# Row maxima of a 64 MB array: contiguous 2 MB loads in place of a 512 KB partition pitch, with the results turned by 32x32 block transposes before the store

## Chip, core and metric

The kernel runs on one core of one Trainium2 chip. The metric is the device time of one execution in microseconds (us). The span of a profile, which is also quoted, runs from the first to the last instruction of that core.

## The reference, cut to what matters

```python
def setup_inputs():
    batch, seq, dim = 32, 512, 1024
    return {"x": np.random.randn(batch, seq, dim).astype(np.float32)}

def reference(x):
    return np.max(x, axis=-1).astype(np.float32)
```

There are 16384 rows of 4 KB, 67.1 MB to read, and one float32 per row to write (64 KB).

## The kernel before

Partition p owns the 128 rows p*128 to p*128+127, which is 512 KB of x. A bulk tile takes four consecutive rows of every partition (16 KB each, 2 MB in all). The last 16 rows of every partition come in eight tiles of 1 MB. The results of a partition are consecutive in the output, so they can be stored as they are.

```python
    I = N // P                                        # 128 rows a partition
    xr = xf.rearrange("(p i) d -> p i d", p=P)        # partition pitch 512 KB
    out_r = bass.AP(tensor=of.tensor, offset=of.offset, ap=[[I, P], [1, I]])
    GB = 4; GT = 2; TAIL_ROWS = 16                    # NB = 28, NT = 8, SPLIT = 112
    # pools: bulk bufs=10, tailp bufs=5, res bufs=1
    # ... (cut)
    for c in range(NB):
        b = c * GB
        xc = bulk.tile([P, GB, D], mybir.dt.float32)
        nc.sync.dma_start(out=xc, in_=xr[:, b:b + GB, :])
        nc.vector.reduce_max(out=res[:, b:b + GB], in_=xc, axis=mybir.AxisListType.X)

    nc.scalar.dma_start(out=out_r[:, :SPLIT], in_=res[:, :SPLIT])       # 56 KB

    for t in range(NT):
        b = SPLIT + t * GT
        xt = tailp.tile([P, GT, D], mybir.dt.float32)
        nc.sync.dma_start(out=xt, in_=xr[:, b:b + GT, :])
        nc.vector.reduce_max(out=res[:, b:b + GT], in_=xt, axis=mybir.AxisListType.X)

    nc.scalar.dma_start(out=out_r[:, SPLIT:], in_=res[:, SPLIT:])       # 8 KB, 64 B runs
```

Of the kernel before, what the change touches and what calls it, by code (L numbers as in the profile page):

```python
# [1 line left out]

# [4 lines left out]


@with_exitstack  # L10
def kernel(
    ctx: ExitStack,
    tc: tile.TileContext,
    x: bass.AP,
    out: bass.AP,
):
    nc = tc.nc
    P = 128

    xf = x.flatten_outer_dims()  # L20
    N, D = xf.shape
    assert N % P == 0
    I = N // P

    xr = xf.rearrange("(p i) d -> p i d", p=P)

    of = out.flatten_outer_dims()
    out_r = bass.AP(tensor=of.tensor, offset=of.offset, ap=[[I, P], [1, I]])

    GB = 4  # L30
    GT = 2
    TAIL_ROWS = 16
    NB = (I - TAIL_ROWS) // GB
    NT = TAIL_ROWS // GT
    SPLIT = I - TAIL_ROWS

    bulk = ctx.enter_context(tc.tile_pool(name="bulk", bufs=10))
    tailp = ctx.enter_context(tc.tile_pool(name="tailp", bufs=5))
    respool = ctx.enter_context(tc.tile_pool(name="res", bufs=1))

    res = respool.tile([P, I], mybir.dt.float32)

    for c in range(NB):
        b = c * GB
        xc = bulk.tile([P, GB, D], mybir.dt.float32)
        nc.sync.dma_start(out=xc, in_=xr[:, b:b + GB, :])  # L46
        nc.vector.reduce_max(  # L47
            out=res[:, b:b + GB],
            in_=xc,
            axis=mybir.AxisListType.X,  # L50
        )

    nc.scalar.dma_start(out=out_r[:, :SPLIT], in_=res[:, :SPLIT])

    for t in range(NT):
        b = SPLIT + t * GT
        xt = tailp.tile([P, GT, D], mybir.dt.float32)
        nc.sync.dma_start(out=xt, in_=xr[:, b:b + GT, :])
        nc.vector.reduce_max(  # L59
            out=res[:, b:b + GT],  # L60
            in_=xt,
            axis=mybir.AxisListType.X,
        )

    nc.scalar.dma_start(out=out_r[:, SPLIT:], in_=res[:, SPLIT:])


# [1 line left out]
_INS = ['x']  # L69
_OUTS = [((32, 512), 'float32')]  # L70


# [23 lines left out]
```

## Time and profile before

| | before |
|---|---|
| time, median of the runs at hand before the change was run | 166.98 us (166.93 to 167.51) |
| span of the profiled execution | 166.5 us |
| read from memory | 67.11 MB, 403 GB/s over the span |
| VectorE (DVE) busy | 141.4 us |
| distance of two bulk reductions, undisturbed | 4.89 us (2.097 MB / 4.89 us = 429 GB/s) |
| one bulk reduction | 4.42 us |

The first lines are of the page of the kernel before: the span, the busy time, the DMA rows in 40 slices of the span (each digit is the busy share of a slice in tenths), and the chain of work that ended last, by engine. SPq, ACTq and DVEq are the instruction queues of SyncE, ScalarE and VectorE; the first two issue the DMAs here.

```profile
span 166.5 us, 142 instructions
DVE 141.4 (85%) x36; POOL 0.2 (0%) x4
...
DMA  5999999999999999999999999999999999999950
GB/s 189 429 441 429 429 394 425 433 437 429 433 421 354 425 433 429 429 429 429 433 421 429 429 429 437 417 429 433 429 433 421 425 433 411 425 417 423 421 222 2
...
DMA 89%; DVE 8%; SPq 1%; issue 0%
```

The DMA engines are busy from the second slice to the last but two, and the chain that ends last is made of loads. Two slices stand out, 394 and 354 GB/s. The timeline of VectorE (start, duration, instruction, and in brackets the idle time ahead of it and what ended it) shows what they are:

```profile
22.90 4.42 DVE L47 TENSOR_REDUCE res<-xc 128x4 f32<-128x4096 f32 x1 [0.47 <-DMA xc<-in_x_dram]
28.43 4.42 DVE L47 TENSOR_REDUCE res<-xc 128x4 f32<-128x4096 f32 x1 [1.11 <-DMA xc<-in_x_dram]
33.29 4.42 DVE L47 TENSOR_REDUCE res<-xc 128x4 f32<-128x4096 f32 x1 [0.44 <-DMA xc<-in_x_dram]
...
52.86 4.42 DVE L47 TENSOR_REDUCE res<-xc 128x4 f32<-128x4096 f32 x1 [0.46 <-DMA xc<-in_x_dram]
58.61 4.42 DVE L47 TENSOR_REDUCE res<-xc 128x4 f32<-128x4096 f32 x1 [1.33 <-DMA xc<-in_x_dram]
63.50 4.42 DVE L47 TENSOR_REDUCE res<-xc 128x4 f32<-128x4096 f32 x1 [0.47 <-DMA xc<-in_x_dram]
```

VectorE always waits for the load, normally 0.47 us. Ahead of two tiles it waits 0.64 and 0.86 us longer, and this is never made good: all later tiles keep the old distance. The end of the same timeline:

```profile
141.82 4.42 DVE L47 TENSOR_REDUCE res<-xc 128x4 f32<-128x4096 f32 x1 [0.48 <-DMA xc<-in_x_dram]
146.16 15.47 DVE L59 TENSOR_REDUCE res<-xt 128x2 f32<-128x2048 f32 x7
...
161.80 2.29 DVE L59 TENSOR_REDUCE res<-xt 128x2 f32<-128x2048 f32 x1 [0.17 <-DMA xt<-in_x_dram]
164.12 0.34 ACTq L65 DMA_DIRECT2D out_dram<-res  x1
```

The last 2 MB tile leaves VectorE with a backlog, so seven tail reductions run without a gap. The eighth waits 0.17 us for its load. One store follows, and the span ends at 166.48 us, 2.36 us after that store's issue began.

### The profile page before, as it was taken

What the parts mean: (1) busy time and instruction counts of PE and PEld (TensorE: products, weight loads), DVE (VectorE), ACT (ScalarE), POOL (GpSimd) and SP (SyncE); (2) the same over time, 40 slices, a digit from 0 to 9 for tenths busy, and PEclk for the clock granted to TensorE, in tenths of its full rate; (3) what the DMA queues carried; (4) which work ended last, traced back from release to release, by engine and by line L of the source; (5) the groups of instructions that cost most, each with busy time, mean ns of one, the idle gap of its engine ahead of it and who ended that gap; (6) DMA issues with size and microseconds to landing.
All of it is one profiled execution on the core that took longest, in us unless ns stands there. A gap on an engine that the chain in (4) does not pass through costs nothing.

```text
span 166.5 us, 142 instructions
## 1 busy us (share of the span) xinstructions
DVE 141.4 (85%) x36; POOL 0.2 (0%) x4
## 2 busy tenths in 40 slices
DVE  0098887898888798888898888899888889999994
POOL 0000000000000000000000000000000000000000
DMA  5999999999999999999999999999999999999950
GB/s 189 429 441 429 429 394 425 433 437 429 433 421 354 425 433 429 429 429 429 433 421 429 429 429 437 417 429 433 429 433 421 425 433 411 425 417 423 421 222 2
DMA packets 5472, 67.18 MB, mean 404 GB/s; under 512 B 864, under 2 KB 864, under 8 KB 864
## 3 DMA queue, kind: packets, MB, share of 16 engines
q1 hardware_dynamic: 5184, 67.11, 95.7%
q10 hardware_dynamic: 288, 0.07, 0.2%
HBM read 67.11 MB, written 0.07 MB: 403 GB/s over the span
## 4 chain that ended last, share of the span: by engine, by line
DMA 89%; DVE 8%; SPq 1%; issue 0%
DMA xc<-in_x_dram 84%; DMA xt<-in_x_dram 5%; DVE res L59 5%; DVE res L47 3%; SPq L46 1%
## 5 line engine op out<-in xcount | busy, mean ns | idle before, releaser
L47 DVE TENSOR_REDUCE res<-xc 128x4 f32<-128x4096 f32 x28 | 123.8, 4420 | 22.5 <-DMA xc<-in_x_dram 22.5
L59 DVE TENSOR_REDUCE res<-xt 128x2 f32<-128x2048 f32 x8 | 17.8, 2280 | 0.2 <-DMA xt<-in_x_dram 0.2
L80 POOL MEMSET const-bfloat16-1.0<- 128x1 bf16 x1 | 0.1, 103 | 0.0
L80 POOL MEMSET const-uint8-127<- 128x1 uint8 x1 | 0.1, 103 | 0.0
L80 POOL MEMSET const-float32-1.0<- 128x1 f32 x1 | 0.1, 100 | 0.0
L80 POOL MEMSET const-float32-0.0<- 128x1 f32 x1 | 0.1, 99 | 0.2 <-issue 0.2
## 6 DMA issues: line engine op xcount, KB each, us to landing
xc<-in_x_dram SPq DMA_DIRECT2D x28, 2048.0 KB, 39.1
xt<-in_x_dram SPq DMA_DIRECT2D x8, 1024.0 KB, 23.5
out_dram<-res ACTq DMA_DIRECT2D x1, 56.0 KB, 6.8
out_dram<-res ACTq DMA_DIRECT2D x1, 8.0 KB, 1.4
```

What stands on the lines that cost most here:

```text
L46: nc.sync.dma_start(out=xc, in_=xr[:, b:b + GB, :])
L47: nc.vector.reduce_max(out=res[:, b:b + GB], in_=xc, axis=mybir.AxisListType.X,)
L59: nc.vector.reduce_max(out=res[:, b:b + GT], in_=xt, axis=mybir.AxisListType.X,)
L80: nc = _bacc.Bacc("TRN2", target_bir_lowering=False, num_devices=1)
```

## The change

Its intent: every bulk load should read one contiguous stretch of 2 MB, and not 128 pieces of 16 KB which lie 512 KB apart (this distance is what I call the pitch). The eight tail loads still read 128 pieces, of 8 KB, now 16 KB apart. The rows of a tile are then spread over the partitions (row = t*512 + p*4 + g), so the four results of one partition and tile are only 16 B of the output. To store longer runs, the results are transposed in blocks of 32x32, after which a partition holds 128 consecutive outputs (512 B), and four stores of 16 KB write them.

```diff
-    xr = xf.rearrange("(p i) d -> p i d", p=P)
+    xr = xf.rearrange("(t p g) d -> t p g d", p=P, g=G)
... (cut)
-        nc.sync.dma_start(out=xc, in_=xr[:, b:b + GB, :])
-        nc.vector.reduce_max(out=res[:, b:b + GB], in_=xc, ...)
+            nc.sync.dma_start(out=xc, in_=xr[t])
+            nc.vector.reduce_max(out=res[:, :, t], in_=xc, axis=X)
+        else:                                # the last four t, in halves
+                nc.sync.dma_start(out=xt, in_=xr[t, :, h:h + 2, :])
+                nc.vector.reduce_max(out=res[:, h:h + 2, t], in_=xt, axis=X)
-    nc.scalar.dma_start(out=out_r[:, :SPLIT], in_=res[:, :SPLIT])
-    nc.scalar.dma_start(out=out_r[:, SPLIT:], in_=res[:, SPLIT:])
+    for g in range(G):
+        nc.vector.transpose(out=turned[:, :, g], in_=res[:, g, :])
+    for q in range(P // 32):
+        dst = bass.AP(tensor=of.tensor, offset=of.offset + q * 32 * G,
+                      ap=[[P * G, T], [1, 32 * G]])
+        eng = (nc.scalar, nc.sync)[q % 2]
+        eng.dma_start(out=dst, in_=turned[q * 32:(q + 1) * 32, :, :].rearrange("p a g -> p (a g)"))
```

Number and size of the loads, bulk before tail, and the number of buffers stay as they were.

More of the change, by code (lines that the diff above doesn't have):

```diff
@@ L7 @@
 from concourse._compat import with_exitstack
+F32 = mybir.dt.float32
+G = 4
 @with_exitstack
@@ L18 @@
     P = 128
+    X = mybir.AxisListType.X
     xf = x.flatten_outer_dims()
     N, D = xf.shape
-    assert N % P == 0
-    I = N // P
-    xr = xf.rearrange("(p i) d -> p i d", p=P)
+    T = N // (P * G)
+    xr = xf.rearrange("(t p g) d -> t p g d", p=P, g=G)
     of = out.flatten_outer_dims()
-    out_r = bass.AP(tensor=of.tensor, offset=of.offset, ap=[[I, P], [1, I]])
-    GB = 4
-    GT = 2
-    TAIL_ROWS = 16
-    NB = (I - TAIL_ROWS) // GB
-    NT = TAIL_ROWS // GT
-    SPLIT = I - TAIL_ROWS
@@ L37 @@
     bulk = ctx.enter_context(tc.tile_pool(name="bulk", bufs=10))
     tailp = ctx.enter_context(tc.tile_pool(name="tailp", bufs=5))
-    respool = ctx.enter_context(tc.tile_pool(name="res", bufs=1))
-    res = respool.tile([P, I], mybir.dt.float32)
-    for c in range(NB):
-        b = c * GB
-        xc = bulk.tile([P, GB, D], mybir.dt.float32)
-        nc.sync.dma_start(out=xc, in_=xr[:, b:b + GB, :])
-        nc.vector.reduce_max(
-            out=res[:, b:b + GB],
-            in_=xc,
-            axis=mybir.AxisListType.X,
-        )
@@ L53 @@
-    nc.scalar.dma_start(out=out_r[:, :SPLIT], in_=res[:, :SPLIT])
-    for t in range(NT):
-        b = SPLIT + t * GT
-        xt = tailp.tile([P, GT, D], mybir.dt.float32)
-        nc.sync.dma_start(out=xt, in_=xr[:, b:b + GT, :])
-        nc.vector.reduce_max(
-            out=res[:, b:b + GT],
-            in_=xt,
-            axis=mybir.AxisListType.X,
-        )
-    nc.scalar.dma_start(out=out_r[:, SPLIT:], in_=res[:, SPLIT:])
+    once = ctx.enter_context(tc.tile_pool(name="once", bufs=1))
@@ new lines @@
+    res = once.tile([P, G, T], F32)
+    turned = once.tile([P, 32, G], F32)
+    for t in range(T):
+        if t < T - 4:
+            xc = bulk.tile([P, G, D], F32)
+            nc.sync.dma_start(out=xc, in_=xr[t])
+            nc.vector.reduce_max(out=res[:, :, t], in_=xc, axis=X)
+        else:
+            for h in range(0, G, 2):
+                xt = tailp.tile([P, 2, D], F32)
+                nc.sync.dma_start(out=xt, in_=xr[t, :, h:h + 2, :])
+                nc.vector.reduce_max(out=res[:, h:h + 2, t], in_=xt, axis=X)
@@ L69 @@
+    for g in range(G):
+        nc.vector.transpose(out=turned[:, :, g], in_=res[:, g, :])
+    for q in range(P // 32):
+        dst = bass.AP(
+            tensor=of.tensor,
+            offset=of.offset + q * 32 * G,
+            ap=[[P * G, T], [1, 32 * G]],
+        )
+        eng = (nc.scalar, nc.sync)[q % 2]
+        eng.dma_start(out=dst, in_=turned[q * 32:(q + 1) * 32, :, :].rearrange("p a g -> p (a g)"))
 _INS = ['x']
```

## The prediction

> **What bounds the kernel now.** The load stream. The page gives 67.11 MB read in a span of 166.5 us; its DMA row is at 9 tenths almost throughout, mostly 421-433 GB/s. In the timeline a 2 MB tile starts its reduction every 4.89 us (428.7 GB/s), while the reduction takes 4.42 us: VectorE idles about 0.47 us before each, always for the load. The chain of waits is 89% DMA. Two tiles are late: the one at 28.43 us by 0.64 us, the one at 58.61 us by 0.86 us (slices of 394 and 354 GB/s), 1.5 us in all. At the end VectorE is almost level with DMA: seven of eight 1 MB tail reductions run back to back, the eighth waits 0.17 us for its load and ends at 164.09 us; then come the 8 KB store (0.34 us issue, 1.4 us to landing) and 2.4 us in all to the end.
>
> **What the change leaves.** Number, size and order of the loads (28 of 2 MB, 8 of 1 MB), bytes per partition and load, buffers, reductions. VectorE's 141.4 us stays within 0.1 us; its 4-result writes become strided, nothing beside 4096 reads.
>
> **What it moves.** The pitch between partitions in x. The Trainium skill, page "DMA: Bandwidth & Descriptors", section "Latency and other measured facts", tells of DRAM copies of 128 x 16 KiB tiles at power-of-two pitches: 207 GB/s at 512 KiB against 214 at full rate, 3%. This trace shows little of that: every undisturbed tile takes 4.89 us to within 0.02 us, which looks like a ceiling of the engines, not like collisions. So I expect 4.87-4.90 us per tile after. What the pitch could own are the two late tiles. I give that a third: gain 1.5 us if so, expected 0.5 us.
>
> **What it removes.** The 56 KB store in the middle of the tail. Both stores together took 0.2% of the 16 engines' time (0.3 us): about 0.2 us off.
>
> **What it adds, all on the critical path, after the last reduction.** Four transposes of 128x32. None is in the trace; estimate from the reductions: 4420 - 2278 = 2142 ns for 2048 elements, so 136 ns fixed and 33 ns for 32 elements, 0.17 us each alone, about 0.09 us overlapped as the tail reductions are: 0.35-0.7 us. Then four 16 KB stores in 512 B runs, two on each of two queues: the second on a queue starts one issue (0.33-0.38 us) later; landing near the 1.4 us of the 8 KB store. Together +0.7 to +1.1 us.
>
> **Sum.** 166.98 + 0.9 - 0.2 - 0.5 = about 167.2 us; range 165.6 to 168.6. Faster by over 2%: 0.03; within 2%: 0.93; slower: 0.04.
>
> **What would show each step.** Timeline: bulk reductions still 4.89 us apart, whether late tiles remain; VectorE's idle time for loads near 22 us (21 if they go). Last reduction ending at 162.5-164.2 us. Four transposes of at most 0.2 us, first store 0.4-0.8 us after the last reduction, second pair about 0.35 us later, end of span 2.6-3.0 us after the first store's issue begins. Chain of waits: DMA still 88-89%.
>
> **What would make it wrong.** If the tile interval itself falls (a collision the same for each tile), to 4.82 us say, the stream gains 2.2 us, with the late tiles gone 3.7 us, just over 2%. If contiguous tiles make the sixteen engines meet in one part of the memory, the interval grows above 4.95 us and the kernel is slower. If transposes or 512 B stores cost 1 us apiece, it is slower by 2-3 us.

## The result, and the profile after

| | before | after |
|---|---|---|
| time, median (lowest to highest), 4 runs each | 166.98 us (166.93 to 167.51) | 168.13 us (168.01 to 168.24) |
| span of the profiled execution | 166.5 us | 166.3 us |
| VectorE busy | 141.4 us | 142.0 us |
| first reduction starts | 8.24 us | 8.58 us |
| last bulk reduction starts | 141.82 us | 140.72 us |
| last reduction ends | 164.09 us | 163.00 us |
| first of the closing stores issued | 164.12 us | 163.39 us |
| from there to the end of the span | 2.36 us | 2.95 us |

The ratio is 1.0059 with a 95% interval of 1.0044 to 1.0074. Ratios in this document are the mean time of one kernel's fast runs over the mean of the other's fast runs of the same rounds, so they are not quite the ratios of the medians that are quoted. The kernel after is slower by about half a per cent, within 2%.

The page of the kernel after, the same lines:

```profile
span 166.3 us, 147 instructions
DVE 142.0 (85%) x40; POOL 0.2 (0%) x4
...
DMA  5999999999999999999999999999999999999930
GB/s 177 402 433 437 441 437 429 410 426 441 433 429 414 426 441 433 426 414 429 441 433 422 422 426 441 433 422 422 426 441 433 422 418 418 422 424 420 422 154 16
...
DMA 83%; DVE 14%; SPq 1%; issue 0%; DVEq 0%
```

The two holes of before are gone. The next lines are of its VectorE timeline, first the start and the stretch in which before had its first late tile, then the end of the timeline of all engines:

```profile
8.58 4.42 DVE L44 TENSOR_REDUCE res<-xc 128x4 f32<-128x4096 f32 x1 [8.58 <-DMA xc<-in_x_dram]
...
23.23 4.42 DVE L44 TENSOR_REDUCE res<-xc 128x4 f32<-128x4096 f32 x1 [0.47 <-DMA xc<-in_x_dram]
28.13 4.42 DVE L44 TENSOR_REDUCE res<-xc 128x4 f32<-128x4096 f32 x1 [0.48 <-DMA xc<-in_x_dram]
```

```profile
140.72 4.42 DVE L44 TENSOR_REDUCE res<-xc 128x4 f32<-128x4096 f32 x1 [0.49 <-DMA xc<-in_x_dram]
145.06 15.44 DVE L49 TENSOR_REDUCE res<-xt 128x2 f32<-128x2048 f32 x7
160.53 0.33 DVE L52 STREAM_TRANSPOSE turned<-res 128x32 f32<-128x32 f32 x2
160.75 2.25 DVE L49 TENSOR_REDUCE res<-xt 128x2 f32<-128x2048 f32 x1
163.03 0.33 DVE L52 STREAM_TRANSPOSE turned<-res 128x32 f32<-128x32 f32 x2
163.39 0.83 SPq L61 DMA_DIRECT2D out_dram<-turned  x2
163.40 0.87 ACTq L61 DMA_DIRECT2D out_dram<-turned  x2
```

Every bulk tile is on time. Two of the transposes were scheduled ahead of the last reduction, because the rows that they turn were complete by then; they fill the 0.17 us in which before waited for its last load, so the last reduction no longer waits for a load, and the chain that ended last runs through VectorE for all eight tail reductions (14% in place of 8%).

Here is the puzzle: **the span fell by 0.14 us, and the time rose by 1.15 us.** The difference can be taken apart by stage from the two traces: first tile 8.58 - 8.24 = +0.34; the 27 further bulk tiles 132.14 - 133.58 = -1.44, nearly all of it the two late tiles; last bulk reduction to the end of the last reduction 22.28 - 22.27 = +0.01; from there to the first store +0.36; from the store to the end +0.59. The sum is -0.14 us. The stages at both ends cost 1.3 us, and the -1.44 us that hides them must be missing from the timed runs.

### The profile page after: what moved, and what is told of

The parts are those of the page before. It is cut to its first block, busy times and chain, and to the rows that moved or that the text cites. A ratio compares the mean times of both kernels' runs of the same rounds, so it can differ in the third digit from the quotient of the medians.

```text
span 166.3 us, 147 instructions
## 1 busy us (share of the span) xinstructions
DVE 142.0 (85%) x40; POOL 0.2 (0%) x4
## 4 chain that ended last, share of the span: by engine, by line
DMA 83%; DVE 14%; SPq 1%; issue 0%; DVEq 0%
DMA xc<-in_x_dram 83%; DVE res L49 11%; DVE res L44 3%; SPq L43 1%; DVE turned L52 0%; DVEq L87 0%
## 5 line engine op out<-in xcount | busy, mean ns | idle before, releaser
L52 DVE STREAM_TRANSPOSE turned<-res 128x32 f32<-128x32 f32 x4 | 0.7, 213 | 0.1
```

The costliest lines, as they stand in the source:

```text
L52: nc.vector.transpose(out=turned[:, :, g], in_=res[:, g, :])
```

## The experiments

Twelve builds were run (before and after again, eight other kernels, two of them twice), each on one chip and with runs of before between them. I call the chips A, B and C. Some kernels are wrong, which their expectation says: loads and end are exchanged separately, so the results land in other places.

| chip | kernel | loads | end | time, median (lowest to highest), runs | ratio to before, 95% interval |
|---|---|---|---|---|---|
| A | before | 512 KB pitch | old | 168.08 (167.47 to 169.16), 11 | |
| A | before, again | 512 KB pitch | old | 167.86 (167.28 to 169.41), 6 | 0.9987, 0.9942 to 1.0031 |
| A | contiguous, old end | contiguous | old | 167.21 (167.13 to 167.37), 6 | 0.9935, 0.9905 to 0.9965 |
| A | old loads, new end | 512 KB pitch | new | 168.81 (168.46 to 169.76), 8 | 1.0029, 0.9995 to 1.0063 |
| A | after, stores on one queue | contiguous | new, ACT only | 168.83 (168.79 to 169.05), 6 | 1.0033, 1.0002 to 1.0063 |
| B | before | 512 KB pitch | old | 166.82 (166.74 to 166.96), 9 | |
| B | after without transposes | contiguous | four stores | 167.56 (167.53 to 167.65), 5 | 1.0044, 1.0031 to 1.0056 |
| B | bulk reversed | 512 KB pitch | old | 166.83 (166.71 to 166.90), 5 | 0.9998, 0.9986 to 1.0011 |
| B | 128 KB pitch | 128 KB pitch | old | 166.44 (166.38 to 166.63), 5 | 0.9978, 0.9966 to 0.9991 |
| B | contiguous, first tile old | mixed | old | 166.82 (166.77 to 167.38), 5 | 0.9997, 0.9984 to 1.0011 |
| C | before | 512 KB pitch | old | 167.27 (166.75 to 167.57), 11 | |
| C | after, again | contiguous | new | 168.06 (167.96 to 168.18), 6 | 1.0053, 1.0038 to 1.0068 |
| C | contiguous, old end, again | contiguous | old | 167.12 (166.98 to 167.29), 6 | 0.9996, 0.9980 to 1.0013 |
| C | old loads, new end, again | 512 KB pitch | new | 167.92 (167.65 to 168.44), 6 | 1.0051, 1.0031 to 1.0071 |
| C | 128 KB pitch, fine tail | 128 KB pitch | old | 165.96 (165.89 to 166.71), 6 | 0.9936, 0.9917 to 0.9955 |

### 1. The kernel before, again

No edit.

> The kernel before, unchanged, under another label, to get span and time of several runs side by side. Theory P (the two late tiles of before belong to the 512 KB pitch): each profile of it shows two tiles 0.5-0.9 us late and the last reduction ending near 164.1 us. Rival N (the late tiles are chance): a second profile shows other tiles late, or none, with the last reduction ending near 162.7 us. The difference of time and span: after has 1.8 us (168.14 against 166.3); if the difference is the same here, spans would be near 165.2 us; if spans are near 166.0-166.5 us, the kernel after has 0.8 us or more outside its span. Ratio 1.000 +-0.002.

Its six runs lie between 167.28 and 169.41 us, and the eleven of the shared kernel before between 167.47 and 169.16. Every one of these runs has a span that is 1.8 us below its time: in the 105 runs that show both, the difference is 1.75 to 1.85 us for every kernel, before and after alike, but for four runs of the last kernel (up to 2.01 us). So nothing of the change lies outside the span, and the rival that said so (L in the next expectation) falls. What was odd was the profile of before: a span of 166.5 us belongs to an execution of about 168.3 us, slower than all its timed runs that I had. The second profile shows two other tiles late, at 37.97 us (by 0.43 us) and at 48.02 us (by 0.26 us). Which tiles are late is chance, as rival N says, but it is not a small matter: on this chip before scatters by 2 us.

```profile
37.97 4.42 DVE L47 TENSOR_REDUCE res<-xc 128x4 f32<-128x4096 f32 x1 [0.90 <-DMA xc<-in_x_dram]
...
48.02 4.42 DVE L47 TENSOR_REDUCE res<-xc 128x4 f32<-128x4096 f32 x1 [0.73 <-DMA xc<-in_x_dram]
```

The DMA packets of the trace show what a late tile is. A 16 KB packet most often takes 0.611 us, and sixteen are in flight on average. These are all packets of at least 4 KB that took over 0.7 us and started later than 7 us after the span began:

```
trace                        number  where (us)           how long (us)
before                          17   19, 23, 51           0.72 to 2.43
before, again                   15   33, 42-44            0.78 to 1.46
old loads, new end              16   23-25, 40            0.72 to 1.91
old loads, new end, again        8   23                   1.16 to 1.76
bulk reversed (chip B)           0
seven with a contiguous bulk      0
128 KB pitch, two traces         0
```

About eight packets at a time are held up, half of those in flight. (Before 7 us every trace has long packets, 16 to 27 of them; the longest is 1.36 to 1.60 us at the two larger pitches and 1.67 to 2.06 us in the seven with a contiguous bulk.) Each load completes in sixteen parts, here called shares, with one event each in the trace, and the reduction waits for the last of them: in the late tile of before it came at 28.41 us, and the reduction began at 28.43 us. In the trace of before the distance between the first and the last share of a tile steps from 0.66 us to 1.29 us at the first event and to 1.74 us at the second, and then stays. In this trace the shares that fell behind do not catch up. This is why a hold-up of some packets once moves the whole rest of the stream.

### 2. Contiguous loads, the old end

```diff
-    xr = xf.rearrange("(p i) d -> p i d", p=P)
+    xr = xf.rearrange("(t p g) d -> t p g d", p=P, g=4)
-        in_=xr[:, b:b + GB, :]
+        in_=xr[c]
-        in_=xr[:, b:b + GT, :]
+        in_=xr[b // 4, :, b % 4:b % 4 + GT, :]
```

> Wrong result on purpose (rows in another order): contiguous 2 MB loads, results and the two stores as before, no transposes. Theory P with an expensive end: 165.5 us (1.5 us less than before, no late tiles, difference of time and span about 1.0 us). Rival N: 167.0 us, as before. Rival L (contiguous loads cost something outside the span): 167.5-168 us with a difference of time and span of 1.8 us.

> Contiguous loads, old end, wrong on purpose, as in the run of that name. If the cost of the new end adds to whatever the loads do: 0.92 us (+-0.1) below the kernel after of the same call. If the contiguous loads have a later first tile on every chip: 0.2-0.4 us above the fastest runs of before of the same call.

On chip A it took 167.21 us with a range of only 0.24 us, while before scattered over 1.7 us beside it. On chip C it took 167.12 us, within a range of 0.31 us, against 166.75 to 167.57 us for before. None of the three readings of the first expectation was right as it stood: the loads do gain, against a before that is held up (ratio 0.9935 on A); they gain nothing against one that is not much so (0.9996 on C); and they lose 0.23 us to before's fastest run on C. The trace on C shows that loss at the start:

```profile
8.55 4.42 DVE L47 TENSOR_REDUCE res<-xc 128x4 f32<-128x4096 f32 x1 [8.55 <-DMA xc<-in_x_dram]
...
160.75 2.29 DVE L59 TENSOR_REDUCE res<-xt 128x2 f32<-128x2048 f32 x1 [0.17 <-DMA xt<-in_x_dram]
163.07 0.34 ACTq L65 DMA_DIRECT2D out_dram<-res  x1
```

In the six traces with contiguous bulk loads throughout the first reduction starts at 8.50 to 8.74 us (the seventh, with another first tile, is experiment 9), in the five at 512 KB pitch at 8.20 to 8.28 us. The steady distance is 4.89 to 4.90 us for both. The 0.17 us wait ahead of the last reduction is back: it belongs to the old end, with its store of 56 KB in the middle of the tail. (The kernel of experiment 8 has a store of only 8 KB there, and its eight tail reductions run without a gap.)

### 3. Old loads, the new end

```diff
 # in the kernel after
-    xr = xf.rearrange("(t p g) d -> t p g d", p=P, g=G)
+    xr = xf.rearrange("(p i) d -> p i d", p=P)
-                in_=xr[t]
+                in_=xr[:, t * G:(t + 1) * G, :]
-                in_=xr[t, :, h:h + 2, :]
+                in_=xr[:, t * G + h:t * G + h + 2, :]
```

> Wrong result on purpose: 512 KB pitch as before, transposes and four stores as after. Theory P with an expensive end: two late tiles, 168.5-169.5 us, difference of time and span near 1.8 us. Rival N: 168.1 us, as after. Rival L: 167.3-168 us with a difference of time and span of 1.0 us.

> 512 KB pitch with transposes and four stores, wrong on purpose. If the two costs add: 0.9 us (+-0.1) above before of the same call on a chip without stalls, and 0.2-0.4 us below the kernel after. On a chip with stalls its runs scatter by 1 us or more as before's do, and the kernel after's do not.

On chip A it scatters from 168.46 to 169.76 us. Its VectorE timeline has the late tiles that the kernel after, with the same end, does not have:

```profile
22.88 4.42 DVE L44 TENSOR_REDUCE res<-xc 128x4 f32<-128x4096 f32 x1 [0.48 <-DMA xc<-in_x_dram]
28.86 4.42 DVE L44 TENSOR_REDUCE res<-xc 128x4 f32<-128x4096 f32 x1 [1.56 <-DMA xc<-in_x_dram]
...
44.48 4.42 DVE L44 TENSOR_REDUCE res<-xc 128x4 f32<-128x4096 f32 x1 [1.43 <-DMA xc<-in_x_dram]
```

So hold-ups follow the loads and not the end. The end's price can be read with the loads held fixed. From the start of the last bulk reduction to the end of the span both traces of this kernel take 25.61 and 25.62 us, the kernel after 25.62 and 25.61 us on its two traces, and the six traces with before's two stores 24.65 to 24.67 us. The new end costs 0.95 us, whatever the loads do. In times of chip C it is 168.06 - 167.12 = 0.94 us with contiguous loads and 167.92 - 167.27 = 0.65 us at the old pitch; the second is blurred by the scatter, and between the fastest runs of each it is 167.65 - 166.75 = 0.90 us.

### 4. After, once more on chip C

No edit.

> The kernel after, unchanged, under another label, to have all four combinations of loads and end on one chip. On a chip whose runs of before do not scatter (before near 166.8 us): 168.0-168.1 us, that is +0.9 us for the end and +0.3 us for the later first tile. On a chip whose runs of before scatter up to 169 us: still 168.0-168.2 us, so no slower than before.

168.06 us, within 0.22 us: as expected, and as in the first comparison. The four corners of the square (two loads, two ends) are now measured on one chip. By the lowest runs they are 166.75 (before), 166.98 (new loads), 167.65 (new end), 167.96 us (both): +0.23 or +0.31 us for the loads, +0.90 or +0.98 us for the end. They add.

### 5. After, with all stores on one queue

```diff
-        eng = (nc.scalar, nc.sync)[q % 2]
+        eng = nc.scalar
```

> The kernel after with all four stores on the ACT queue. If the extra time outside the span comes from storing on two queues, the difference of time and span falls from 1.8 us to about 1.0 us; the span grows by two more issues one after the other, 0.7-0.8 us, so that the time is about 168.0-168.2 us. If it does not come from the two queues, time 168.7-169.0 us.

168.83 us, as its second reading expected, on chip A, where the kernel after was not run; against its 168.13 and 168.06 us elsewhere it is 0.7 to 0.8 us slower, the size of two further issues. The end of its timeline:

```profile
162.97 0.33 DVE L52 STREAM_TRANSPOSE turned<-res 128x32 f32<-128x32 f32 x2
163.33 1.78 ACTq L61 DMA_DIRECT2D out_dram<-turned  x4
```

Four issues take 1.78 us one after the other, against 0.83 and 0.87 us side by side; from the first issue to the end of the span it is 3.66 us against 2.95 us. Two queues are the better way to send four stores, and the number of stores one after the other on a queue is part of the price. The Trainium skill says in "DMA: Bandwidth & Descriptors", section "Issuing engines are not separate DMA queues", that issuing from several engines saves only the sequencer's issue time, usually small beside the DMA itself. This trace agrees on what is saved (0.71 us of span), and at the very end of this kernel, behind the last data, even that counts.

### 6. After, without its transposes

```diff
-    for g in range(G):
-        nc.vector.transpose(out=turned[:, :, g], in_=res[:, g, :])
-        eng.dma_start(out=dst, in_=turned[q * 32:(q + 1) * 32, :, :].rearrange("p a g -> p (a g)"))
+        eng.dma_start(out=dst, in_=res[q * 32:(q + 1) * 32, :, :].rearrange("p g t -> p (g t)"))
```

> The kernel after, its four transposes left out, the four stores taken from the untransposed results: wrong on purpose. Theory E (the new end costs 0.36 us through the transposes that stand between the last reduction and the first store, and 0.5 us through the stores): 0.5-0.6 us below the kernel after (two of the transposes also stand ahead of the last reduction, 0.22 us), so about 167.5-167.6 us; last reduction to start of first store 0.03 us; from there to the end of the span still 2.9 us. Rival S (the stores are nearly all of it): less than 0.2 us below the kernel after, about 168.0 us.

167.56 us, 0.50 to 0.57 us below the kernel after (on other chips; both kernels repeat within 0.25 us). Theory E holds, rival S falls. The end:

```profile
158.14 4.68 DVE L48 TENSOR_REDUCE res<-xt 128x2 f32<-128x2048 f32 x2
162.85 0.82 SPq L57 DMA_DIRECT2D out_dram<-res  x2
162.85 0.86 ACTq L57 DMA_DIRECT2D out_dram<-res  x2
```

The stores start 0.03 us after the last reduction in place of 0.39 us, and from there to the end it is 2.94 us, unchanged from after and 0.58 us longer than with the single 8 KB store of before. From the last bulk reduction to the end of the span this kernel takes 25.14 us, 0.48 us less than after and 0.48 us more than before. So the 0.95 us of the new end is half transposes and half stores. (For the stores it is 0.58 us less 0.1 us: with the store in the middle of the tail gone, and no transposes, the last reduction ends 0.1 us sooner after the last bulk reduction began, 22.18 us in place of 22.28 us.)

### 7. The old loads with the bulk reversed

```diff
-    for c in range(NB):
+    for c in reversed(range(NB)):
```

> The kernel before with its 28 bulk tiles loaded in reverse order; the result is correct. In the traces at 512 KB pitch so far, eight engines at a time had packets of 0.75-2.4 us in place of 0.61 us, at 23 and 51 us, at 33 and 42-44 us, at 23 and 40 us, never after 52 us. Theory T (the stalls belong to the time since the start): long packets again between 20 and 55 us only. Rival A (they belong to addresses, the first rows of each 512 KB): long packets between 85 and 130 us. Both: spans scatter over 1.5 us or more, as before, median time 167.5-168.5 us.

This run tells nothing about its question. On chip B there is no sign of hold-ups: before took 166.74 to 166.96 us in nine runs, this kernel 166.71 to 166.90 us, and its trace has no long packet after 7 us. Whether hold-ups belong to the time since the start or to addresses stays open. The run is of use all the same: its trace is the one at 512 KB pitch without a late tile, with a span of 165.04 us. That execution took 166.85 us, and the undisturbed before of the same chip took 166.82 us.

### 8. A pitch of 128 KB, the old end

```diff
-    I = N // P
-    xr = xf.rearrange("(p i) d -> p i d", p=P)
+    U = 4
+    I = N // P // U
+    xr = xf.rearrange("(u p i) d -> u p i d", u=U, p=P)
 # loop over u around the loop over bulk tiles; one store of 128 B runs after each of
 # the first three u; the last u has two stores of 64 B runs, its last 16 rows as before
```

> A correct kernel between the two: x in four groups of 4096 rows, partition pitch 128 KB in each, so results go out in 64-128 B runs without transposes, the last store as before. If the stalls need the pitch of 512 KB (or its 64 MB spread): no long packets after the first 6 us, runs within 0.4 us of each other, 167.1-167.3 us as with contiguous loads and the old end. If a pitch of 128 KB is enough for stalls: runs scatter over 1 us or more, median 167.5-168.2 us.

This kernel is correct, has no transposes, and took 166.44 us, ratio 0.9978 with an interval below 1. That is below both ranges that I had expected, neither of which foresaw an earlier first tile and a shorter end. Two lines of its timeline:

```profile
8.11 4.42 DVE L48 TENSOR_REDUCE res<-xc 128x4 f32<-128x4096 f32 x1 [8.11 <-DMA xc<-in_x_dram]
...
162.55 0.34 ACTq L64 DMA_DIRECT2D out_dram<-res  x1
```

Its first tile is the earliest of this chip (8.11 us against 8.28 us of before's loads), the closing store comes at 162.55 us against 162.68 us, and from there to the end it takes 2.20 us against 2.36 us. The shares of its first tile land within 0.51 us, against 0.74 us for the old pitch on the same chip and 0.70 us for contiguous loads. Its steadiness proves nothing, since before was as steady on this chip.

### 9. Contiguous, with only the first tile at the old pitch

```diff
 # in the kernel of experiment 2
-        in_=xr[c]
+        in_=xr[c] if c else xold[:, 0:GB, :]      # xold: the 512 KB pitch
```

> Contiguous loads with the old end (167.21 us on the chip of its run), only the very first tile read at the 512 KB pitch; wrong on purpose. If the 0.3-0.5 us by which the first tile lands later in contiguous loading (8.5-8.7 us against 8.2 us) come from the first tile's own pitch: first reduction at 8.2 us and time 166.8-166.9 us, the lowest yet. If they come from the next tiles that are in flight at the same time: first reduction at 8.5 us or later and time 167.1-167.3 us.

Inconclusive. Four of five runs took 166.77 to 166.85 us, as the first reading says and as before did. But the fifth, 167.38 us, is the profiled one, and it has the latest first tile of all traces:

```profile
8.78 4.42 DVE L49 TENSOR_REDUCE res<-xc 128x4 f32<-128x4096 f32 x1 [8.78 <-DMA xc<-in_x_dram]
```

There were no late tiles after that one, so all of its 0.6 us come from the start. The four good runs have no trace. So the times of four runs speak for the first reading and the only trace speaks against it. Whether the pitch of the first tile sets the start is not shown.

### 10. 128 KB pitch and a finer tail

In all kernels so far at least one reduction of a 1 MB tile is left to do when the last load lands: in before it lands at 161.78 us and its reduction ends 2.31 us later. This one keeps the 128 KB pitch and takes the last 12 MB as eight loads of 1 MB and eight of 512 KB.

```diff
-    TAIL_ROWS = 16
+    TAIL_ROWS = 24
+    LAST_ROWS = 8
+        pieces = [(b, GT, tailp) for b in range(split, I - LAST_ROWS, GT)]
+        pieces += [(b, 1, lastp) for b in range(I - LAST_ROWS, I)]
 # pools: bulk bufs=9, tailp bufs=4, lastp bufs=6; the middle store after the first 16 rows
```

> Correct kernel: pitch of 128 KB with the old end (166.44 us, 0.998 of before), and the last 12 MB in eight loads of 1 MB and eight of 512 KB in place of eight of 1 MB. The tail reductions of all kernels run back to back and the last one ends 2.3 us after the last load; with smaller last tiles VectorE should end about 1.2-1.4 us after it. Packets of 8 KB took 0.309 us against 0.611 us for 16 KB (1% more per byte), 4 KB packets should cost a little more: 0.2-0.4 us for 12 MB. Expected 165.6-165.9 us, ratio 0.993-0.995. If VectorE does not catch up (its idle before the last tile stays 0), or the small packets cost over 1 us: 166.4 us or more.

It is correct and the fastest: 165.96 us, ratio 0.9936 on chip C, just outside the expected 165.6 to 165.9 us. Part of that ratio is before's own scatter there; between the fastest runs it is 166.75 - 165.89 = 0.86 us. One of its six runs was 166.71 us, and it has no trace, so a hold-up in that run is not ruled out.

```profile
158.15 3.59 DVE L65 TENSOR_REDUCE res<-xt 128x1 f32<-128x1024 f32 x3
161.77 0.34 ACTq L70 DMA_DIRECT2D out_dram<-res  x1
```

The last load lands at 160.50 us and VectorE is done at 161.74 us, 1.24 us later in place of 2.31 us. The small packets give part of it back: a 4 KB packet most often takes 0.159 us, where a quarter of 0.611 us would be 0.153 us, and the last load lands 0.29 us later than in experiment 8 although the first tile was 0.14 us earlier.

## Why the prediction was right, and where its terms were off

The time, 168.13 us, lies in the range of 165.6 to 168.6 us, and "within 2%" was right. Both leave much room: the range is 3 us wide, and 2% is 3.3 us. The point, 167.2 us, was 0.9 us too low, and the missed terms below all erred in the same direction, so the range held in spite of them. One of the signs asked for did not come: the chain of waits has DMA at 83%, not 88 to 89%. Term by term:

- **The tile interval** was predicted to stay at 4.87 to 4.90 us, and stayed: 4.89 to 4.90 us at a pitch of 512 KB, 128 KB and 16 KB. A 16 KB packet took 0.611 us most often in every trace, and 0.612 to 0.614 us in the median, and sixteen packets of 16 KB in 0.611 us are 429 GB/s. The Trainium skill's 207 against 214 GB/s at a pitch of 512 KiB ("DMA: Bandwidth & Descriptors", "Latency and other measured facts"), told of copies between two DRAM tensors, does not show in the steady state of this load stream.
- **The new end**, predicted at +0.7 to +1.1 us, measured +0.95 us: 0.48 us by the transposes (0.213 us each on average, a little above the predicted 0.2 us), 0.48 us by the stores (experiments 3 and 6). Right. The prediction's "all on the critical path, after the last reduction" was not quite so: two transposes ran ahead of the last reduction. They were on the critical path all the same, since VectorE had no gap there but the 0.17 us which they filled.
- **"About 0.2 us off"** for the store in the middle of the tail gave nothing: from the start of the last bulk reduction to the end of the last one it takes 22.27 us before and 22.28 us after. Without transposes it is 22.18 us (experiment 6), so the removal is worth 0.1 us, and the two early transposes use it up. Before's tail still ended on a load, by 0.17 us; without the 56 KB store it belongs to VectorE.
- **"I give that a third: gain 1.5 us if so, expected 0.5 us"** is the term that failed, and its baseline more than its odds. The late tiles do belong to the loads: they vanish with them. But they come and go by run and by chip, and the time from which I subtracted them, 166.98 us, hardly held any. An undisturbed before takes 166.8 us (experiment 7), so there was 0.1 to 0.2 us to gain in three of those four runs, not 1.5. I read the stages from one execution of about 168.3 us and the sum from others. On chip A, where before's median is 168.08 us, the gain was real, about 0.9 us for the loads alone (experiment 2). I did not run the kernel after there; as an estimate, 167.21 us plus 0.95 us for its end is 168.2 us, level with before.
- **The first tile** was not in the sum at all. It lands 0.2 to 0.5 us later with contiguous loads, +0.34 us in the two traces compared, and nothing in the trace of after makes that delay good: its later tiles keep the steady distance.

The corrected sum: 166.98 + 0.95 (end) + 0.34 (first tile) - 0.15 (late tiles) = 168.1 us, as measured. What stays open is why half of the packets in flight are held up, by 0.1 to 1.8 us, at the 512 KB pitch, in four of its five traces (not in the one from chip B), in the first third of the run, and why the start is later when the loads are contiguous. The measurements show which loads have it, and no run shows the mechanism.

## What to carry to other kernels

Before taking a gain off a measured time, make sure that the profile that shows the gain is of an execution like the timed ones: compare the span with the span of several timed runs. Here the steady distance of the tiles was the same at pitches of 16, 128 and 512 KB, while what followed the last load was paid in full (0.95 us of span, 0.94 us of time), so a layout that needs a transpose and more stores at the end has to win their microsecond back somewhere. A middle way may need no such end: here a pitch of 128 KB keeps the results in order, and smaller last tiles then shorten what VectorE has left to do after the last load.

## What the Trainium skill lacked or had wrong

- "DMA: Bandwidth & Descriptors", "Latency and other measured facts", on row pitches: no run here shows a steady loss at 512 KiB for loads into SBUF (most often 0.611 us a packet of 16 KB, as at 128 KB and 16 KB). What it lacks are sporadic hold-ups of about eight packets at a time, 0.72 to 2.43 us in place of 0.611 us, in four of five traces at the 512 KB pitch and in none of nine at smaller pitches (the one without, and three of the nine, are from chip B). They spread the runs of a kernel over up to 2.1 us, where kernels with contiguous loads throughout stayed within 0.31 us.
- The same page, on the sixteen shares of a DMA: it lacks that in these streams a share which had fallen behind stayed behind to the end. In before the shares of a tile landed within 0.66 us, then 1.29 us, then 1.74 us, and 1.7 us to the end; each step delayed all later tiles.
- No page has the gap between these two measures: the span from the first to the last instruction was 1.75 to 2.01 us shorter than the device time in the 105 runs that show both, so either can be worked out from the other to within 0.3 us.
- "VectorE: DVE Perf Modes", "The three transpose paths", gives 311 ns for a 128x128 bf16 transpose on VectorE and no time for a smaller one: four 32x32 blocks of fp32 (128x32) took 0.192 to 0.235 us here.
